# Order of high-part and low-part matmuls within a weight piece, and the place of the first down projection's last turns

## The chip, the core and the metric

The kernel runs on one core of one Trainium2 chip. The metric is the time of one execution on the device in microseconds (us), as the median of three runs; less is better. The engines of the core have queues of their own: TensorE multiplies matrices (PE in the profile; its weight loads are PEld), VectorE (DVE) and ScalarE (ACT) do elementwise work, GpSimd (POOL) and SyncE (SP) mostly issue DMA transfers. TensorE writes to PSUM, a memory of eight banks of 512 float32 per partition; everything else lies in SBUF.

## What is computed

The reference is a decoder trunk of two layers on one sequence of 256 tokens with 2048 features: a gated linear attention layer, then an attention layer over one block of shared keys and values, each followed by a gated feed-forward network with a short convolution.

```python
for layer in range(DEPTH):                     # DEPTH = 2
    if layer < N_A_LAYERS:
        h = h + gla_mixer(h, ...)
    else:
        if layer == N_A_LAYERS:
            k_blk, v_blk, k_mean = shared_kv(h, kv_norm, kv_w, k_norm_w)
        h = h + moba_mixer(h, ..., k_blk, v_blk, k_mean, rel_bias)
    h = h + conv_ffn(h, ...)                   # rms_norm, w_up, conv, silu(a) * u, w_down
```

Nearly all of the work is products of activations (256 tokens) with weight matrices: 2048 inputs to the several projections, 2048 to 2 x 5632 in each up projection, 5632 to 2048 in each down projection. All data is float32.

## The kernel before

**High and low parts.** Each float32 operand is used as a sum of two numbers of the matmul's input type: a high part (the rounded value) and a low part (what the rounding left). A product of two such operands is made of three: high x high, high x low, low x high. The activations lie as `[128, 2 * S]` per k-tile, high part in the first 256 columns, low part in the next 256 (`make_xw`, line 221). The weights come as pieces of `[128, 1024]` float32, half of a chunk of 2048 columns.

**The weight stream** (`WeightStream`, line 55). Chunks of 1 MB are fetched by DMAs on the SP queue into three buffers (`wraw`). For each piece ACT casts the high part (`whi`, line 126) and DVE subtracts it from the original to get the low part (`wlo`, line 127). There are three buffers each for `whi` and `wlo`, and pieces are prepared two ahead of the one in use. `step()` (line 289) hands out the next piece, and ahead of that runs the jobs that were put off with `after(n, job)` until n steps later.

**`gemm`** (line 298) has the weights as the stationary operand and the activations as the moving one. One step holds 4 k-tiles x 2 output blocks. For each of these 8 tiles there is one 512-wide matmul with `whi` against both parts of the activation (line 307), and one 256-wide matmul with `wlo` against the high part alone (line 308). It runs for the key, query, gate and output projections of the first layer, for both up projections, and for the output projection of the second layer: 120 calls of four steps, 480 steps in all. In the last step of a call the tiles of output block 0 come first.

**`gemm_tok`** (line 312) has the activations as the stationary operand and the weights as the moving one, three 512-wide matmuls per tile (lines 323 to 325): x high with w high, x high with w low, x low with w high. It makes the values of the first layer, and queries, keys and values of the second.

**`down`** (line 626) is the down projection, in two column blocks. Most input pairs use a scheme with seven products rather than eight of 2 x 2 blocks (`seven`), with sums and differences of weights and activations (`t13`, `t24` on DVE in `_sums`, lines 99 to 101; `comb` for the activations). `prod` (line 646) does one product as three 512-wide matmuls, in the order x high w high, x high w low, x low w high (line 653). Of a pair with seven products, the four weight pieces hold 1, 2, 2 and 2 of them. The results p1 to p8 lie in PSUM banks; p4 and p8 are in the two banks of the `bank` pool, the others in pairs in the `acc_ps` pool of three. The last pairs of a block (the tail) are run once per half `f`, and after each half `sums(f, ...)` adds the results to their buffers.

**The turns** (`back`, line 770). The first down projection gives its result with tokens on partitions; the kernel goes on with features on partitions. `back(q)` transposes block q of eight with four matmuls against the identity (line 777), adds it to the residual stream `h[q]` (line 779) and feeds the norm: `make_xw` (two casts on ACT, line 225, and two operations on DVE, line 227) and the square and its sum (lines 237 and 238). Turns 0 to 3 stand in the second block of `down`, turn 4 in its tail at (1, 1), all of them into an `acc_ps` tile, 5 to 7 in steps 1 to 3 of the first `gemm_tok` call of the queries, into the `bank` pool; `nrm.close`, which makes the norm's factor for each token, stands at step 4. Step q of that call uses the operand of turn q.

The program order is not the last word: a scheduler with a simulated timeline places the instructions on the queues of the engines, within what the data dependencies allow.

Of the kernel before, what the change touches and what calls it, by code (L numbers as in the profile page):

```python
# [8 lines left out]
F32 = mybir.dt.float32  # L9
# [9 lines left out]
S = 256  # L19
KT = D // 128  # L20
NP = KT // 2
# [121 lines left out]
def trunk(ctx: ExitStack, tc: tile.TileContext, xT, cst, msk, w1p, w2a, w_k, w_qa, w_v2, w_v, w_g, w_go,  # L143
          w_up0, w_dn0, w_kk, w_kv, w_mq, w_mo, w_up1, w_dn1, rel, onehot, out):
    nc = tc.nc
    V, A, T = nc.vector, nc.scalar, nc.tensor
# [7 lines left out]
    acc_ps = ctx.enter_context(tc.tile_pool(name="acc_ps", bufs=3, space=PSUM))  # L154
# [9 lines left out]
    def bank(name, shape):  # L164
        return mis_ps.tile(list(shape), F32, name=name, tag="bank")
# [117 lines left out]
    cur = [0]  # L283
    later = []

    def after(steps, job):
        later.append((cur[0] + steps, job))

    def step():
        due = [job for at, job in later if at <= cur[0]]  # L290
        later[:] = [(at, job) for at, job in later if at > cur[0]]
        for job in due:
            job()
        halves_ = ws.get(cur[0])
        cur[0] += 1
        return halves_

    def gemm(xs, kts):
        ps = acc_ps.tile([128, 2, 512], F32, name="acc")
        for q0 in range(0, kts, 4):  # L300
            hi, lo = step()
            order = [(k, b) for k in range(4) for b in range(2)]
            for k, b in sorted(order, key=lambda kb: kb[1]) if q0 == kts - 4 else order:
                kt = q0 + k
                x = xs(kt)
                c = k * 256 + b * 128
                T.matmul(ps[:, b, :], hi[:, c:c + 128], x, start=kt == 0, stop=False)  # L307
                T.matmul(ps[:, b, :S], lo[:, c:c + 128], x[:, :S], start=False, stop=kt == kts - 1)  # L308
        ws.prefetch(cur[0])
        return ps  # L310

    def gemm_tok(xs, groups=1):
        out_ = [acc_ps.tile([128, 2, 512], F32, name="acc") for _ in range(groups)]
        for q0 in range(0, KT, 2):
            for ps in out_:
                hi, lo = step()
                for k in range(2):
                    kt = q0 + k
                    x = xs(kt)
                    wh, wl = hi[:, k * 512:(k + 1) * 512], lo[:, k * 512:(k + 1) * 512]  # L320
                    for t in range(2):
                        xh, xl = x[:, 128 * t:128 * t + 128], x[:, S + 128 * t:S + 128 * t + 128]
                        T.matmul(ps[:, t, :], xh, wh, start=kt == 0, stop=False)  # L323
                        T.matmul(ps[:, t, :], xh, wl, start=False, stop=False)  # L324
                        T.matmul(ps[:, t, :], xl, wh, start=False, stop=kt == KT - 1)  # L325
        ws.prefetch(cur[0])
        return out_ if groups > 1 else out_[0]

# [41 lines left out]
    nrm = Norm(C_GN, "xw", columns=True)  # L370
# [7 lines left out]
    xs = rows(nrm.xs)  # L378
# [247 lines left out]
    def down(layer, hid, ready, jobs):  # L626

        def late(k):
            return lambda: combine_parts(k, hid)

        done = set(EARLY)
        for b, order in enumerate(ORDERS[layer]):
            new = [k for k, seven in order if seven and k not in done]
            done |= set(new)
            todo = dict(jobs.get(b, {}))
            for i, k in enumerate(new):
                todo.setdefault(2 + 2 * i, []).append(late(k))
            low = acc_ps.tile([128, 2, 512], F32, name="acc")
            p = {2: low[:, 0], 3: low[:, 1], 4: bank("p4", (128, 512)), 8: bank("p8", (128, 512))}
            left = dict.fromkeys(range(1, 9), 0)  # L640
            for k, seven in order:
                for n in ((1, 5, 7, 6, 4, 3, 2) if seven else (2, 3, 4, 8, 2, 3, 4, 8)):
                    left[n] += 3
            begun = set()

            def prod(n, x, w, f):
                hi, lo = (t[:, 512 * f:512 * f + 512] for t in w)
                if n not in p:
                    two = acc_ps.tile([128, 2, 512], F32, name="acc")
                    p.update({n: two[:, 0], {1: 6, 5: 7}[n]: two[:, 1]})  # L650
                for xp, wp in ((x[0], hi), (x[0], lo), (x[1], hi)):
                    left[n] -= 1
                    T.matmul(p[n], xp, wp, start=n not in begun, stop=left[n] == 0)  # L653
                    begun.add(n)

            def part(k, i, t):
                x = hid[k][:, i, 128 * t:]
                return x[:, :128], x[:, S:S + 128]

            def comb(k, f):  # L660
                return combos[k][:, f, 0], combos[k][:, f, 1]

            last = max(i for i, (k, seven) in enumerate(order) if seven)
            tail = [k for k, _ in order[len(order) - _tail(order):]]
            for i, (k, seven) in enumerate(order[:len(order) - len(tail)]):
                for job in todo.get(i, ()):
                    job()
                if seven:
                    prod(1, part(k, 0, 0), step(), 0)
                    w = step()  # L670
                    prod(3, comb(k, 3), w, 0)
                    prod(2, part(k, 1, 0), w, 1)
                    w = step()
                    prod(5, comb(k, 0), w, 0)
                    prod(7, comb(k, 2), w, 1)
                    w = step()
                    prod(6, comb(k, 1), w, 0)
                    prod(4, part(k, 1, 1), w, 1)
                else:
                    for a in range(2):  # L680
                        w = step()
                        for n, t, f in ((2, 0, a), (3, 0, 1 - a), (4, 1, a), (8, 1, 1 - a)):
                            prod(n, part(k, a, t), w, f)
                if i == last:
                    sums = ready(b, p)
            for f, (n0, n1) in enumerate(((2, 4), (3, 8))):
                for i, k in enumerate(tail):
                    for job in todo.get((f, i), ()):
                        job()
                    w = step()  # L690
                    todo_ = [(n, t, a) for a in range(2) for n, t in ((n0, 0), (n1, 1))]
                    for n, t, a in sorted(todo_, key=lambda x: x[1]) if i == len(tail) - 1 else todo_:
                        prod(n, part(k, a, t), w, a)
                if f:
                    ws.prefetch(cur[0])
                sums(f, (n0, n1))
# [61 lines left out]
    def first_down(hid, nrm):  # L758
        blocks = {}

        def ready(b, p):
            blocks[b] = r = u_sums(p, None)

            def end(c, ns):
                for t, n in enumerate(ns):
                    V.tensor_add(r[2 * t + c], r[2 * t + c], p[n])

            return end

        def back(q, where):  # L770

            r = blocks[q // 4]
            tp = where()
            c, i0 = q % 4 // 2, q % 2 * 2
            for i in range(2):
                for t in range(2):
                    T.transpose(tp[:, i, 128 * t:128 * t + 128],
                                r[2 * t + c][:, 128 * (i0 + i):128 * (i0 + i) + 128], ident)
            V.tensor_add(h[q], h[q], tp)
            nrm.feed(q)  # L780

        def load_back(m):
            hs[m] = slot([128, 2, 2, S], F32, "h")
            for q in (2 * m, 2 * m + 1):
                h[q] = hs[m][:, q % 2]
                nc.gpsimd.dma_start(h[q], hspill[q].rearrange("a (b c) -> a b c", b=2))

        pair = []

        def in_acc():  # L790
            if not pair:
                two = acc_ps.tile([128, 2, 512], F32, name="acc")
                pair.extend(two[:, i].rearrange("p (a b) -> p a b", a=2) for i in range(2))
            return pair.pop(0)

        jobs = {2: [lambda q=q: back(q, in_acc) for q in (0, 1)]}
        for q, i in ((2, 3), (3, 4), (4, (1, 1))):
            jobs.setdefault(i, []).append(lambda q=q: back(q, in_acc))
        for m, i in enumerate((0, 1, 15, 16)):
            jobs.setdefault(i, []).append(lambda m=m: load_back(m))  # L800
        down(0, hid, ready, {1: jobs})
        for q in (5, 6, 7):
            after(q - 4, lambda q=q: back(q, lambda: bank("hf", (128, 2, S))))
        after(4, nrm.close)

    n_ffn = Norm(C_FN, "xw")
    project(rows(go), KT, [n_ffn])
# [254 lines left out]
```

## Time and profile before

| what | value |
|---|---|
| median of three runs | 2245.56 us (2244.91 to 2245.88) |
| profiled execution, its own time | 2244.39 us |
| its span, first to last instruction | 2242.6 us |
| PE busy | 2226.1 us |
| DVE busy | 1659.1 us |
| ACT busy | 1260.5 us |
| matmuls | 11776 |

The profile is of one execution. Its page has the busy time of each engine, the span in 40 slices, the DMA queues, the chain of work that ended last (followed back from the last instruction to what released it), and the groups of instructions that cost most. Other views list the waits by who waited for whom, the instructions in order of time, and the sums over chosen windows of time. A row of instructions reads: start in us, duration in us, engine, line of the kernel, operation, tile written <- tiles read, shape. The duration of a matmul includes its way through the pipeline, so matmuls overlap in the rows: what a matmul costs in a stream is the distance from its start to the start of the next.

### The profile page before, as it was taken

To read this page: it belongs to the slowest core of one execution; us is meant where nothing else is said; L and a number is where in the kernel's file an instruction comes from. 1 tells how busy PE (TensorE), PEld (TensorE's weight loads), DVE (VectorE), ACT (ScalarE), POOL (GpSimd) and SP (SyncE) were. 2 spreads that over 40 slices of the span, in tenths; PEclk is the share of its full clock that TensorE was granted. 3 is DMA by queue.
4 is the path that set the end of the run, shared out by engine and by line. 5 is a ranking of instruction groups with operands and counts; after the bars stand their busy time and mean duration, and the time that the engine had idled before them with its cause. 6 is when DMAs were issued, how large, how long until landed. Compare 5 with 4: busy or idle time off the path is not lost.

```text
span 2242.6 us, 30203 instructions
## 1 busy us (share of the span) xinstructions
PE 2226.1 (99%) x11776; PEld 1901.9 (85%) x11776; DVE 1659.1 (74%) x2279; ACT 1260.5 (56%) x1754; POOL 44.1 (2%) x60
## 2 busy tenths in 40 slices
PE   8999999999999999999999999999999999999999
PEld 7889888888888888887788888888888888887877
DVE  6666776777777777978867666567777777788886
ACT  6655644655555555555556565456555555555553
POOL 0000000000000000000001000000000000000000
PEclk9999999999999999999999999999999999999999
DMA  6554556555555555555656554456655555556654
GB/s 257 188 188 135 172 194 210 191 188 188 188 188 187 184 183 198 197 196 192 226 185 218 177 169 158 165 191 205 202 188 188 189 189 192 192 195 209 242 194 146
DMA packets 63297, 428.50 MB, mean 191 GB/s; under 512 B 7553, under 2 KB 8081, under 8 KB 13106
## 3 DMA queue, kind: packets, MB, share of 16 engines
q1 hardware_dynamic: 59346, 415.43, 53.8%
q0 software_dynamic: 3232, 10.56, 1.4%
q8 instruction: 92, 1.51, 0.3%
q10 hardware_dynamic: 576, 0.58, 0.1%
q14 instruction: 51, 0.42, 0.1%
HBM read 420.23 MB, written 6.32 MB: 190 GB/s over the span
## 4 chain that ended last, share of the span: by engine, by line
PE 91%; DVE 4%; DMA 3%; issue 1%; ACT 1%; DVEq 0%; ACTq 0%
PE acc L307 40%; PE acc L308 20%; PE acc L653 8%; PE p L653 5%; PE acc L324 5%; PE acc L325 5%; PE acc L323 5%; DMA wraw<-w_dn 3%; DVE wlo L127 2%; ACT whi L126 1%; DVE t L99 1%; PE sT L511 0%; DMA wraw<-w_v 0%; PE tr L856 0%; PE s L874 0%
## 5 line engine op out<-in xcount | busy, mean ns | idle before, releaser
L127 DVE TENSOR_TENSOR wlo<-wraw,whi 128x1024 fp32r<-128x1024 f32 (+1 forms) x785 | 937.4, 1200 | 452.5 <-ACT whi L126 445.9
L126 ACT CAST whi<-wraw 128x1024 fp32r<-128x1024 f32 (+1 forms) x785 | 807.2, 1033 | 791.9 <-PE acc L307 465.8
L307 PE MATMUL acc<-xw,whi 128*128 128x512 f32 x3328 | 1168.4, 396 | 0.0
L308 PE MATMUL acc<-xw,wlo 128*128 128x256 f32 x3328 | 933.8, 281 | 0.0
L307 PEld LDWEIGHTS acc<-xw,whi 128*128 128x128 f32 x3328 | 624.2, 188 | 146.8
L308 PEld LDWEIGHTS acc<-xw,wlo 128*128 128x128 f32 x3328 | 628.8, 189 | 0.2
L653 PE MATMUL acc<-whi,hid 128*128 128x512 f32 x576 | 204.9, 390 | 0.1
L653 PE MATMUL p<-whi,hid 128*128 128x512 f32 x512 | 179.7, 390 | 0.0
L653 PEld LDWEIGHTS acc<-whi,hid 128*128 128x128 f32 x576 | 108.1, 188 | 22.8 <-ACT whi L126 0.5
L126 ACT CAST whi<-t 128x1024 fp32r<-128x1024 f32 x64 | 67.4, 1054 | 85.1 <-PE p L653 75.9
L653 PE MATMUL acc<-wlo,hid 128*128 128x512 f32 x288 | 113.0, 393 | 1.0 <-DVE wlo L127 0.8
L653 PEld LDWEIGHTS p<-whi,hid 128*128 128x128 f32 x512 | 96.1, 188 | 20.1
L323 PE MATMUL acc<-whi,xw 128*128 128x512 f32 x256 | 101.2, 396 | 5.0 <-ACT xw L225 5.0
L324 PE MATMUL acc<-wlo,xw 128*128 128x512 f32 x256 | 101.3, 396 | 0.9 <-DVE wlo L127 0.9
L324 PE MATMUL acc<-wlo,xkv 128*128 128x512 f32 x256 | 100.6, 393 | 0.0
L323 PE MATMUL acc<-whi,xkv 128*128 128x512 f32 x256 | 100.6, 393 | 0.0
L325 PE MATMUL acc<-whi,xw 128*128 128x512 f32 x256 | 100.5, 392 | 0.0
L325 PE MATMUL acc<-whi,xkv 128*128 128x512 f32 x256 | 100.4, 392 | 0.0
L610 ACT ACTIVATE au<-up,cs 128x256 f32<-128x256 f32 x176 | 96.0, 593 | 7.1 <-DVE up L606 7.1
L653 PE MATMUL p<-wlo,hid 128*128 128x512 f32 x256 | 99.7, 389 | 0.0
L127 DVE TENSOR_TENSOR wlo<-t,whi 128x1024 fp32r<-128x1024 f32 x64 | 77.9, 1222 | 23.7 <-ACT whi L126 23.3
L307 PE MATMUL acc<-go,whi 128*128 128x512 f32 x256 | 90.5, 399 | 0.0
(260 smaller groups left out, 2359.1 us busy)
## 6 DMA issues: line engine op xcount, KB each, us to landing
wraw<-w_up SPq DMA_DIRECT2D x176, 1024.0 KB, 4.8
wraw<-w_dn SPq DMA_DIRECT2D x88, 1024.0 KB, 4.9
wraw<-w_g SPq DMA_DIRECT2D x16, 1024.0 KB, 4.9
wraw<-w_go SPq DMA_DIRECT2D x16, 1024.0 KB, 4.8
wraw<-w_mq SPq DMA_DIRECT2D x16, 1024.0 KB, 4.8
wraw<-w_kk SPq DMA_DIRECT2D x16, 1024.0 KB, 4.8
wraw<-w_kv SPq DMA_DIRECT2D x16, 1024.0 KB, 4.8
wraw<-w_mo SPq DMA_DIRECT2D x16, 1024.0 KB, 4.8
```

Of the source, the lines that this page charges most:

```text
L99: V.tensor_sub(t13, src[:, 512:1536], src[:, 0:1024])
L126: nc.scalar.copy(hi[:, a:b], src[:, a:b])
L127: nc.vector.tensor_sub(lo[:, a:b], src[:, a:b], hi[:, a:b].bitcast(F32))
L307: T.matmul(ps[:, b, :], hi[:, c:c + 128], x, start=kt == 0, stop=False)
L308: T.matmul(ps[:, b, :S], lo[:, c:c + 128], x[:, :S], start=False, stop=kt == kts - 1)
L323: T.matmul(ps[:, t, :], xh, wh, start=kt == 0, stop=False)
L324: T.matmul(ps[:, t, :], xh, wl, start=False, stop=False)
L325: T.matmul(ps[:, t, :], xl, wh, start=False, stop=kt == KT - 1)
L610: A.activation(au[:, i, :], t[:, i, :], AF.Identity, bias=col(cb + n), scale=col(cw + 2 * 2 * FT + n))
L653: T.matmul(p[n], xp, wp, start=n not in begun, stop=left[n] == 0)
```

## The change

There are two parts. First, within each weight piece the matmuls with the high part of the weights all come ahead of those with the low part, in `gemm`, `gemm_tok` and `down`. In the last step of a `gemm` call this is done for output block 0 and then for block 1. In the first step of the program (`cur[0] == 1`) of `gemm_tok` it is done for each k-tile by itself. In `down`, `prods` takes all products of one piece and runs x high w high for all of them, then x low w high, then x high w low; the order by `t` in the last tail step is gone. Second, turn 4 moves from the tail of the first down projection to step 1 of the queries, turns 5 to 7 and the closing of the norm move back by one step each, and turn 4 now goes into the `bank` pool.

```diff
@@ gemm
-            order = [(k, b) for k in range(4) for b in range(2)]
-            for k, b in sorted(order, key=lambda kb: kb[1]) if q0 == kts - 4 else order:
-                kt = q0 + k
-                x = xs(kt)
-                c = k * 256 + b * 128
-                T.matmul(ps[:, b, :], hi[:, c:c + 128], x, start=kt == 0, stop=False)
-                T.matmul(ps[:, b, :S], lo[:, c:c + 128], x[:, :S], start=False, stop=kt == kts - 1)
+            for bs in ((0,), (1,)) if q0 == kts - 4 else ((0, 1),):
+                tiles_ = [(q0 + k, b, k * 256 + b * 128) for k in range(4) for b in bs]
+                for kt, b, c in tiles_:
+                    T.matmul(ps[:, b, :], hi[:, c:c + 128], xs(kt), start=kt == 0, stop=False)
+                for kt, b, c in tiles_:
+                    T.matmul(ps[:, b, :S], lo[:, c:c + 128], xs(kt)[:, :S], start=False, stop=kt == kts - 1)
@@ gemm_tok
-                for k in range(2):
...
-                        T.matmul(ps[:, t, :], xh, wh, start=kt == 0, stop=False)
-                        T.matmul(ps[:, t, :], xh, wl, start=False, stop=False)
-                        T.matmul(ps[:, t, :], xl, wh, start=False, stop=kt == KT - 1)
+                for ks in ((0,), (1,)) if cur[0] == 1 else ((0, 1),):
+                    tiles_ = [(q0 + k, t, k * 512) for k in ks for t in range(2)]
+                    for x0 in (0, S):
+                        for kt, t, c in tiles_:
+                            T.matmul(ps[:, t, :], xs(kt)[:, x0 + 128 * t:x0 + 128 * t + 128], hi[:, c:c + 512],
+                                     start=kt == 0 and x0 == 0, stop=False)
+                    for kt, t, c in tiles_:
+                        T.matmul(ps[:, t, :], xs(kt)[:, 128 * t:128 * t + 128], lo[:, c:c + 512],
+                                 start=False, stop=kt == KT - 1)
@@ down
-            def prod(n, x, w, f):
-                hi, lo = (t[:, 512 * f:512 * f + 512] for t in w)
...
-                for xp, wp in ((x[0], hi), (x[0], lo), (x[1], hi)):
-                    left[n] -= 1
-                    T.matmul(p[n], xp, wp, start=n not in begun, stop=left[n] == 0)
-                    begun.add(n)
+            def prods(*todo):
+
+                w = step()
+                for n, _, _ in todo:
+                    if n not in p:
+                        two = acc_ps.tile([128, 2, 512], F32, name="acc")
+                        p.update({n: two[:, 0], {1: 6, 5: 7}[n]: two[:, 1]})
+                for xi, wi in ((0, 0), (1, 0), (0, 1)):
+                    for n, x, f in todo:
+                        left[n] -= 1
+                        T.matmul(p[n], x[xi], w[wi][:, 512 * f:512 * f + 512], start=n not in begun, stop=left[n] == 0)
+                        begun.add(n)
...
-                    todo_ = [(n, t, a) for a in range(2) for n, t in ((n0, 0), (n1, 1))]
-                    for n, t, a in sorted(todo_, key=lambda x: x[1]) if i == len(tail) - 1 else todo_:
-                        prod(n, part(k, a, t), w, a)
+                    prods(*((n, part(k, a, t), a) for a in range(2) for n, t in ((n0, 0), (n1, 1))))
@@ first_down
-        for q, i in ((2, 3), (3, 4), (4, (1, 1))):
+        for q, i in ((2, 3), (3, 4)):
...
-        for q in (5, 6, 7):
-            after(q - 4, lambda q=q: back(q, lambda: bank("hf", (128, 2, S))))
-        after(4, nrm.close)
+        for q in range(4, NP):
+            after(q - 3, lambda q=q: back(q, lambda: bank("hf", (128, 2, S))))
+        after(5, nrm.close)
```

More of the change, by code (lines that the diff above doesn't have):

```diff
@@ L316, in gemm_tok @@
                 hi, lo = step()
-                for k in range(2):
[L318 to L325, printed above, removed]
+                for ks in ((0,), (1,)) if cur[0] == 1 else ((0, 1),):
[7 more added lines that the diff above has]
+                                 start=False, stop=kt == KT - 1)
         ws.prefetch(cur[0])
@@ L644, in down @@
             begun = set()
-            def prod(n, x, w, f):
-                hi, lo = (t[:, 512 * f:512 * f + 512] for t in w)
-                if n not in p:
-                    two = acc_ps.tile([128, 2, 512], F32, name="acc")
-                    p.update({n: two[:, 0], {1: 6, 5: 7}[n]: two[:, 1]})
-                for xp, wp in ((x[0], hi), (x[0], lo), (x[1], hi)):
-                    left[n] -= 1
-                    T.matmul(p[n], xp, wp, start=n not in begun, stop=left[n] == 0)
-                    begun.add(n)
+            def prods(*todo):
[9 more added lines that the diff above has]
+                        begun.add(n)
             def part(k, i, t):
@@ L668, in down @@
                 if seven:
[L669 to L678, printed above, removed]
+                    prods((1, part(k, 0, 0), 0))
+                    prods((3, comb(k, 3), 0), (2, part(k, 1, 0), 1))
+                    prods((5, comb(k, 0), 0), (7, comb(k, 2), 1))
+                    prods((6, comb(k, 1), 0), (4, part(k, 1, 1), 1))
                 else:
                     for a in range(2):
-                        w = step()
-                        for n, t, f in ((2, 0, a), (3, 0, 1 - a), (4, 1, a), (8, 1, 1 - a)):
-                            prod(n, part(k, a, t), w, f)
+                        prods(*((n, part(k, a, t), f)
+                                for n, t, f in ((2, 0, a), (3, 0, 1 - a), (4, 1, a), (8, 1, 1 - a))))
                 if i == last:
@@ L689, in down @@
                         job()
-                    w = step()
-                    todo_ = [(n, t, a) for a in range(2) for n, t in ((n0, 0), (n1, 1))]
-                    for n, t, a in sorted(todo_, key=lambda x: x[1]) if i == len(tail) - 1 else todo_:
-                        prod(n, part(k, a, t), w, a)
+                    prods(*((n, part(k, a, t), a) for a in range(2) for n, t in ((n0, 0), (n1, 1))))
                 if f:
```

## The prediction

> **What bounds the kernel now.** I read the page first: engine shares, the slices, the chain that ended last, the costliest groups.
>
> ```profile
> span 2242.6 us, 30203 instructions
> ...
> PE 2226.1 (99%) x11776; PEld 1901.9 (85%) x11776; DVE 1659.1 (74%) x2279; ACT 1260.5 (56%) x1754; POOL 44.1 (2%) x60
> ...
> PEclk9999999999999999999999999999999999999999
> ...
> PE 91%; DVE 4%; DMA 3%; issue 1%; ACT 1%; DVEq 0%; ACTq 0%
> ...
> L307 PE MATMUL acc<-xw,whi 128*128 128x512 f32 x3328 | 1168.4, 396 | 0.0
> L308 PE MATMUL acc<-xw,wlo 128*128 128x256 f32 x3328 | 933.8, 281 | 0.0
> ```
>
> TensorE matmul is busy 99% at full granted clock, 91% of the chain is its own, and its idle time is 2242.6 - 2226.1 = 16.5 us. The change keeps the number of matmuls. So it can act in two ways only: through the distance from one matmul to the next (the means of 396 and 281 ns overlap, they are not that distance), and through those 16.5 us.
>
> For the distance I took windows over two stages in which `gemm` runs almost alone, and divided time by the count of PE.
>
> ```profile
> core 0: us, PE busy (x) PEld busy (x) DVE busy (x) ACT busy (x) POOL busy (x), PEclk, DMA share, GB/s
> 240.00:880.00 640.00, 640.00 (x3627) 555.08 (x3626) 477.63 (x674) 360.53 (x499) 4.37 (x8) 1.00 0.56 190
> 1600.00:1960.00 360.00, 360.00 (x2079) 317.40 (x2078) 276.45 (x405) 206.40 (x296) 0.00 (x0) 1.00 0.56 190
> ```
>
> 640/3627 = 176.5 ns and 360/2079 = 173.2 ns per matmul: a pair of one 512-wide (high) and one 256-wide (low) matmul takes 353 ns in the first stage and 346 ns in the second, at the same clock. The alternating order therefore has at least two rhythms. A step of `gemm` has 8 pairs: 2.82 us or 2.77 us.
>
> For the idle time I asked the list of waits, and the groups of PE by form.
>
> ```profile
> ACT whi L126 <- PE p L653: 136.1, 86, 4.8
> ...
> DVE t L99 <- DMA wraw<-w_dn: 20.8, 16, 3.5
> ...
> PEld acc L653 <- DVE wlo L127: 12.8, 19, 1.6
> ...
> PE acc L653 <- DVE wlo L127: 5.6, 9, 1.1
> ```
>
> ```profile
> L653 PE MATMUL acc<-wlo,hid 128*128 128x512 f32 x288 | 113.0, 393 | 1.0 <-DVE wlo L127 0.8
> L324 PE MATMUL acc<-wlo,xw 128*128 128x512 f32 x256 | 101.3, 396 | 0.9 <-DVE wlo L127 0.9
> ...
> L653 PE MATMUL acc<-wlo,comb 128*128 128x512 f32 x128 | 50.8, 397 | 4.9 <-DVE wlo L127 4.9
> ```
>
> The stalls of TensorE outside the start are waits for the low part `wlo`, in the two down projections. That is where a later use of the low part can pay.
>
> **The change part by part. 1: gemm, 480 steps.** (16 k-tiles of 4 per step, 120 calls: 4+4+8+8+44 up to the first up projection, 8+44 later; 272 steps in the first rhythm, 208 in the second.) Eight alternating pairs become a run of eight 512-wide and a run of eight 256-wide matmuls. No instruction is added or removed; what is unknown is the distance inside the runs. The trace has both kinds of run elsewhere: the value matmuls (256-wide) that the queue put together, and `gemm_tok` matmuls (512-wide) right after 256-wide ones.
>
> ```profile
> 1398.15 0.28 PE L394 MATMUL o<-p,vm 128*128 128x256 f32 x1
> ...
> 1398.87 0.40 PE L324 MATMUL acc<-wlo,xkv 128*128 128x512 f32 x1
> ```
>
> ```profile
> 1406.66 0.28 PE L394 MATMUL o<-p,vm 128*128 128x256 f32 x1
> ...
> 1407.13 0.28 PE L396 MATMUL o<-p,vm 128*128 128x256 f32 x1
> ```
>
> ```profile
> 33.35 2.46 PE L417 MATMUL z<-xw,w1s 128*128 128x512 f32 x10
> ```
>
> ```profile
> 70.76 0.40 PE L431 MATMUL gk<-zst,w2t 81*128 81x256 f32 x2
> 71.00 0.40 PE L324 MATMUL acc<-wlo,xw 128*128 128x512 f32 x1
> ...
> 71.47 0.39 PE L323 MATMUL acc<-whi,xw 128*128 128x512 f32 x1
> ...
> 72.39 0.39 PE L324 MATMUL acc<-wlo,xw 128*128 128x512 f32 x1
> 72.62 0.39 PE L325 MATMUL acc<-whi,xw 128*128 128x512 f32 x1
> ```
>
> ```profile
> 920.46 2.27 PE acc L653 x10
> ```
>
> The low run: from 1398.15 six 256-wide ones, each with its own weight load, take 0.72 us (120 ns each); from 1406.66 four take 0.47 us (117 ns). Standing together costs nothing extra. Eight take 0.94 to 0.96 us, I take 0.95. The high run: right after a 256-wide matmul the 512-wide ones are slow at first (71.00 to 71.47: two distances of 235 ns) and then quiet (10 in 2.27 us in the chain of waits, 227 ns). Seven distances from 71.00 to 72.62 take 1.62 us, with an eighth of 0.23 it is 1.85; the ten from 33.35, also behind a narrow one, take 2.46 - 0.39 for nine distances, 230 ns, so 1.84 for eight. I take 1.845. A grouped step is 1.845 + 0.95 = 2.795 us. Against the first rhythm (2.823) that is -0.028 x 272 = -7.6 us, against the second (2.771) +0.024 x 208 = +5.0 us: the two nearly cancel, **-3 us** in all. Bound below: quiet throughout, 8 x (0.227 + 0.117) = 2.752, which against the mean of before, 2.800, is -0.048 x 480 = -23 us. Bound above: never quiet, 8 x (0.235 + 0.120) = 2.840, +0.040 x 480 = +19 us.
>
> The Trainium skill (TensorE: Matmul & The Clock Gate, "LDWEIGHTS (loading the stationary operand)") gives a weight load as columns / 1.2 in ns, by that an estimate of 107 ns for 128 columns, about as long as a 256-wide matmul streams, and in "Back-to-back issue gap" N/2.4 + 2.5 ns per matmul. By both, each matmul costs the same in either order (an estimate of 8 x 216 + 8 x 109 = 2.60 us per step), so part 1 would bring 0; the trace's 2.82 and 2.77 for the same work at the same clock do not agree with one fixed cost.
>
> **2: gemm_tok and down.** All their matmuls are 512-wide and stay so; rhythm unchanged, 0 us. No row shows this new order among equal widths; the quiet 227 ns of the chain and the 230 ns of the run at 33.35 are 3 ns apart, and a third of that on 3552 matmuls bounds it at -3.6 and +3.6 us (an estimate). What moves is the waiting. In a six-matmul step of `down` the low part was wanted second (high, low, high per product), now it is wanted fifth: three matmuls later, 3 x 0.23 = 0.68 us; in a step of three, 0.23 us. And `whi` is free for ACT after the fourth matmul rather than the sixth, while ACT waits 136.1 us in 86 times for just that. The 12.8 us in 19 waits are on average 0.67 us, the longest 1.6 us: most would vanish, the long ones halve. But PE's own idle time there is 4.9 + 1.0 = 5.9 us, and DVE's wait for w_dn (20.8 us, 16 times) stands ahead of some of them, which the order doesn't touch: what is late next is the sum `t` behind that DMA. I take **-5 us** (bounds 0, when the DMA sets the pace, and -12.8). In the first step of the program (`cur[0] == 1`), and at the end of the values, the 0.9 us of L324 shrink: **-0.4 us** (0 to -0.9).
>
> A new wait can arise where `down` passes to its second block: all four x-high products stand first, so the first use of bank p8 comes fourth, 3 x 0.23 = 0.68 us into the block, instead of tenth. The bank is read by the closing additions, as at the end of the kernel:
>
> ```profile
> 2237.63 0.39 PE L653 MATMUL p<-whi,hid 128*128 128x512 f32 x1
> 2237.83 0.69 DVE L745 TENSOR_TENSOR res<-res,acc 128x512 f32<-128x512 f32 x1 [7.25 <-PE acc L653]
> 2238.44 0.68 DVE L745 TENSOR_TENSOR res<-res,p 128x512 f32<-128x512 f32 x1
> ```
>
> The second addition ends at 2239.12, the first slot after the last matmul is 2237.86: 1.26 us, less 0.68 that lies beside matmuls: 0.6 us per passage, two passages; behind it stand all matmuls of the block. The queue may put ready products ahead, so I take **+0.6 us** (0 to +1.2). The dropped sorting of the last tail step costs nothing at the end: here too the last two matmuls belonged to different sums.
>
> **3: the moved turns.** Turn 4 goes from the tail to step 1 of the queries, 5 to 7 and the closing of the norm one step later each. No DMA is issued by them; the SP and POOL queues keep their order.
>
> ```profile
> 1135.50 0.87 DVE L227 SCALAR_TENSOR_TENSOR xw<-h,cs,xw 128x256 fp32r<-128x256 f32 x2
> 1135.56 0.59 PEld L777 LDWEIGHTS hf<-mk,c 128*128 128x128 f32 x4
> 1135.79 0.60 PE L777 MATMUL hf<-mk,c 128*128 128x128 f32 x4
> 1136.04 1.05 ACT L126 CAST whi<-wraw 128x1024 fp32r<-128x1024 f32 x1
> 1136.43 0.69 DVE L779 TENSOR_TENSOR h<-h,hf 128x512 f32<-128x512 f32 x1
> 1137.03 0.68 DVE L238 TENSOR_TENSOR acc_sq<-acc_sq,hsq 128x512 f32<-128x512 f32 x1
> ...
> 1137.63 1.22 DVE L127 TENSOR_TENSOR wlo<-wraw,whi 128x1024 fp32r<-128x1024 f32 x1
> ...
> 1146.48 0.64 PEld L272 LDWEIGHTS sum_h<-one,acc_sq 128*128 128x128 f32 x4
> ...
> 1151.54 0.68 ACT L840 ACTIVATE hsq<-acc,col_h 128x512 f32<-128x512 f32 x1
> ```
>
> PE's four transposes take the same 4 x 0.11 us in either place. DVE pays 0.69 + 0.87 + 0.68 = 2.24 us per turn beside a `wlo` of 1.22: 3.46 us in a step of 12 x 0.227 = 2.72 us, so it falls 0.74 us behind per turn, 3.0 us over four. The operand of turn q is wanted three steps later (8.2 us), so the lag is covered; without the cover it would be the 3.0 us. The sums for the closing ran 5 us ahead of the head norm (1146.5 to 1151.5) and may go 2.7 us later. **0 us** (0 to +3).
>
> Sum: -3 - 5 - 0.4 + 0.6 + 0 = -7.8. The profiled execution took 2244.39 us (span 2242.6 and 1.8 around it): 2236.6. The median of the runs is 2245.56, 1.2 above: **2238 us**.
>
> **The rivals.** A: the runs are quiet throughout, 2.75 per step: 2245.6 - 23 - 4.8 = 2218. The 227 and 117 ns do occur; against it, both quoted 512-wide runs behind a narrow matmul need some matmuls first. B: the mean distance doesn't depend on the order, only the waits fall: 2245.6 - 4.8 = 2241; against it stand the two rhythms of one and the same order. (B is what the rule of the Trainium skill above comes to.) C: it doesn't do what it says: the queue's order is made by a scheduler which already pulled high matmuls forward (at 2237.41 and 2237.63 two high ones end different sums), or the DMA sets the pace in down and the stalls only move: 2245. D, slower: the 512-wide ones never quiet down, because a narrow run follows every eight: 2.84 per step, 2245.6 + 19 - 4.8 = 2260; it turns slower by more than 0.2% from 2.82 per step on. For it, the first distances after a narrow run are 235 ns; against it, they fall within the seven that the rows show. E, slower: the turns in the queries come late, each up to one step of 2.72 us: +11, 2249 with the other gains; against it the 8.2 us of lead.
>
> **How the numbers follow.** Forecast 47%, A 15%, B 10%, C 8%, D 15%, E 5%. 0.2% (4.5 us) is about what this kernel's measurement can tell. Faster: 42 of the forecast's 47, A 15, half of B: 0.62. Within: 5, 5 and C's 8: 0.18. Slower: D and E: 0.20. The forecast's own range is 2230 to 2243 (stalls from -12.8 to 0 at the other terms' values); the range reaches into A and D until two in ten are out: 2222 to 2256.
>
> **What would show it.** Right: windows 240 to 880 and 1600 to 1960 give the same time per matmul, near 175 ns (2.795/16); the timeline shows eight L-high then eight L-low; `PEld acc <- DVE wlo` falls from 12.8 below 6 us; no wait of PE for h or xw in the queries. Wrong: a time per matmul above 176 ns in both stages (D), below 173 (A), PE idle unchanged at 16.5 us (C).

## The result and the profile after

| | before | changed |
|---|---|---|
| median | 2245.72 us (2244.91 to 2246.40, 4 runs) | 2228.85 us (2227.11 to 2229.33, 4 runs) |
| ratio | | 0.9924, 95% interval 0.9906 to 0.9941 |
| span of the profiled execution | 2242.6 us | 2227.3 us |

The changed kernel is faster by 16.9 us in the medians and by 15.3 us in the two profiled spans. The forecast was 2238 us, a gain of 8: the direction and the range (2222 to 2256) hold, the size is about half of what came.

First the page of the changed kernel, with busy times, chain, the two groups of `gemm` (L305, L307) and the first of `gemm_tok` (L320).

```profile
span 2227.3 us, 30386 instructions
...
PE 2217.3 (100%) x11776; PEld 1908.2 (86%) x11776; DVE 1647.8 (74%) x2279; ACT 1266.6 (57%) x1754; POOL 44.1 (2%) x60
...
PE 96%; DMA 2%; DVE 1%; issue 1%; ACT 0%; DVEq 0%; ACTq 0%
...
L305 PE MATMUL acc<-xw,whi 128*128 128x512 f32 x3328 | 854.4, 393 | 0.0
...
L307 PE MATMUL acc<-xw,wlo 128*128 128x256 f32 x3328 | 481.6, 282 | 0.0
...
L320 PE MATMUL acc<-whi,xw 128*128 128x512 f32 x512 | 130.2, 395 | 5.1 <-ACT xw L225 5.1
```

The idle time of PE fell from 16.5 to 2227.3 - 2217.3 = 10.0 us; half of that is the 5.1 us in which the first matmul waits for the first activation (L320). The busy time of L305 looks 314 us smaller than that of L307 of before (1168.4), yet no work left: a group's busy time is the time that its own matmuls cover, overlaps counted once, and eight of a kind in a row overlap one another, where before each overlapped its neighbours of the other line. It can't be used for what a matmul costs; the windows can, with the same two stretches as before:

```profile
core 0: us, PE busy (x) PEld busy (x) DVE busy (x) ACT busy (x) POOL busy (x), PEclk, DMA share, GB/s
240.00:880.00 640.00, 640.00 (x3664) 562.39 (x3663) 478.35 (x684) 367.73 (x505) 4.37 (x8) 1.00 0.56 191
1600.00:1960.00 360.00, 360.00 (x2062) 316.37 (x2061) 270.23 (x399) 206.69 (x292) 0.00 (x0) 1.00 0.55 188
```

640/3664 = 174.7 and 360/2062 = 174.6 ns per matmul: one rhythm in both stages, 349.2 ns per pair, 2.79 us per step. The prediction had 2.795 us and 174.7 ns. The first stage gained on 176.5, the second lost on 173.2.

The timeline of PE shows the runs of eight (an `x8` row is eight matmuls merged, its duration goes from the first start to the last end):

```profile
600.50 2.00 PE L305 MATMUL acc<-xw,whi 128*128 128x512 f32 x8
602.34 1.11 PE L307 MATMUL acc<-xw,wlo 128*128 128x256 f32 x8
603.29 2.00 PE L305 MATMUL acc<-xw,whi 128*128 128x512 f32 x8
```

Eight high ones from 600.50 to 602.34 take 1.84 us, eight low ones from 602.34 to 603.29 take 0.95: the two terms that the prediction read from other matmuls.

The waits, and the groups of PE by form that read a low part:

```profile
ACT whi L126 <- PE p L655: 88.1, 63, 4.4
...
DVE t L99 <- DMA wraw<-w_dn: 27.6, 16, 4.0
...
ACT whi L126 <- PE acc L655: 23.2, 29, 3.5
...
PEld acc L655 <- DVE wlo L127: 2.7, 6, 0.9
```

```profile
L655 PE MATMUL acc<-wlo,hid 128*128 128x512 f32 x288 | 95.7, 390 | 0.6 <-DVE wlo L127 0.5
...
L323 PE MATMUL acc<-wlo,xw 128*128 128x512 f32 x256 | 70.2, 394 | 0.0
...
L655 PE MATMUL acc<-wlo,comb 128*128 128x512 f32 x128 | 44.4, 390 | 0.1
```

The wait of the weight loads for the low part went from 12.8 to 2.7 us, below the 6 that the prediction named as its sign. The idle time ahead of the low parts went from 4.9 + 1.0 + 0.9 = 6.8 us to 0.7. DVE waits longer for the weights of the down projection than before (27.6 instead of 20.8 us), and TensorE hardly feels it.

Where the 15.3 us of span came from, by the starts of the first matmul of each stage in the two timelines:

| stage | before, us | changed, us | difference |
|---|---|---|---|
| start, values, keys, queries, gate | 300.99 | 298.26 | -2.7 |
| output projection, first layer | 90.46 | 89.46 | -1.0 |
| first up projection | 497.71 | 492.45 | -5.3 |
| first down, queries, keys, values | 531.19 | 525.71 | -5.5 |
| output projection, second layer | 91.27 | 91.78 | +0.5 |
| second up projection | 492.45 | 495.99 | +3.5 |
| second down, to the end | 238.53 | 233.65 | -4.9 |

### The profile page after: what moved, and what is told of

It reads as the page before. It is cut to its first block, busy times and chain, and to the rows that moved or that the text cites. A ratio compares the mean times of both kernels' runs of the same rounds, so it can differ in the third digit from the quotient of the medians.

```text
span 2227.3 us, 30386 instructions
## 1 busy us (share of the span) xinstructions
PE 2217.3 (100%) x11776; PEld 1908.2 (86%) x11776; DVE 1647.8 (74%) x2279; ACT 1266.6 (57%) x1754; POOL 44.1 (2%) x60
## 4 chain that ended last, share of the span: by engine, by line
PE 96%; DMA 2%; DVE 1%; issue 1%; ACT 0%; DVEq 0%; ACTq 0%
PE acc L305 40%; PE acc L307 21%; PE acc L655 11%; PE acc L320 11%; PE p L655 7%; PE acc L323 5%; DMA wraw<-w_dn 2%; DVE wlo L127 1%; PE sT L510 0%; PE tr L848 0%; PE s L866 0%; PE pT L886 0%; DVE t L100 0%; PE z L416 0%; PE s L864 0%
## 5 line engine op out<-in xcount | busy, mean ns | idle before, releaser
L305 PE MATMUL acc<-xw,whi 128*128 128x512 f32 x3328 | 854.4, 393 | 0.0
L305 PEld LDWEIGHTS acc<-xw,whi 128*128 128x128 f32 x3328 | 590.8, 189 | 98.8
L307 PEld LDWEIGHTS acc<-xw,wlo 128*128 128x128 f32 x3328 | 468.4, 190 | 41.7
L307 PE MATMUL acc<-xw,wlo 128*128 128x256 f32 x3328 | 481.6, 282 | 0.0
L320 PE MATMUL acc<-whi,xw 128*128 128x512 f32 x512 | 130.2, 395 | 5.1 <-ACT xw L225 5.1
L320 PE MATMUL acc<-whi,xkv 128*128 128x512 f32 x512 | 133.6, 394 | 0.0
L320 PEld LDWEIGHTS acc<-whi,xw 128*128 128x128 f32 x512 | 96.4, 190 | 25.1 <-ACT xw L225 5.1
L320 PEld LDWEIGHTS acc<-whi,xkv 128*128 128x128 f32 x512 | 94.3, 188 | 18.4
L655 PE MATMUL acc<-whi,comb 128*128 128x512 f32 x256 | 83.4, 389 | 0.0
L613 DVE SCALAR_TENSOR_TENSOR au<-up,cs,au 128x254 f32<-128x254 f32 x176 | 77.3, 477 | 0.0
L611 DVE SCALAR_TENSOR_TENSOR au<-up,cs,au 128x255 f32<-128x255 f32 x176 | 76.8, 477 | 0.0
```

What stands on the lines that cost most here:

```text
L305: T.matmul(ps[:, b, :], hi[:, c:c + 128], xs(kt), start=kt == 0, stop=False)
L307: T.matmul(ps[:, b, :S], lo[:, c:c + 128], xs(kt)[:, :S], start=False, stop=kt == kts - 1)
L320: T.matmul(ps[:, t, :], xs(kt)[:, x0 + 128 * t:x0 + 128 * t + 128], hi[:, c:c + 512], start=kt == 0 and x0 == 0, stop=False)
L611: V.scalar_tensor_tensor(au[:, i, 1:], t[:, i, :S - 1], col(cw + 2 * FT + n), au[:, i, 1:], op0=OP.mult, op1=OP.add)
L613: V.scalar_tensor_tensor(au[:, i, 2:], t[:, i, :S - 2], col(cw + n), au[:, i, 2:], op0=OP.mult, op1=OP.add)
L655: T.matmul(p[n], x[xi], w[wi][:, 512 * f:512 * f + 512], start=n not in begun, stop=left[n] == 0)
```

## The experiments: each part by itself

The first four kernels are the kernel before with one part of the diff each (the hunks are those shown with the change).

**Only gemm.** The hunk of `gemm` alone.

> The kernel before with the new order in gemm alone. Theory (each part of the change works by itself): a gemm step is 2.795 us wherever it stands, so 640 us from 240 to 880 hold about 3664 matmuls and 360 us from 1600 to 1960 about 2062; the stages up to the first down get 9 us shorter, those of the second layer's output and up projections 4 us longer, sum -5 us: about 2241; the waits of the down projections stay (PEld acc on DVE wlo 12 to 13 us). Rival (all of the gain is rhythm, also carried into the down projections): 2229 to 2233.

Measured: 2242.58 us, before 2246.77 on the same chip, ratio 0.9982 (0.9973 to 0.9992); span 2239.7. Its windows and its list of waits:

```profile
240.00:880.00 640.00, 640.00 (x3666) 562.35 (x3666) 477.33 (x682) 368.86 (x505) 4.39 (x8) 1.00 0.56 191
1600.00:1960.00 360.00, 360.00 (x2062) 316.28 (x2061) 271.89 (x402) 208.35 (x294) 0.00 (x0) 1.00 0.55 188
```

```profile
PEld acc L652 <- DVE wlo L127: 13.2, 18, 1.9
```

The counts are as expected to two matmuls, the waits in the down projections are untouched. By stages: -7.7 us up to the first down, +4.0 in the second layer: -3.7 us; by the medians -4.2. The rival, that the rhythm makes all of the gain, falls.

**Only down.** The hunk of `down` alone.

> The kernel before with the new order in down alone. Theory: the gain of the two down projections (5.5 and 4.9 us in the trace of the changed kernel) is of the order of parts: -10 us, about 2235, waits of PEld acc on DVE wlo below 4 us, gemm unchanged at 2.82 and 2.77 us per step. Rival (half of it came from the turn that left the tail, or from the phase in which the gemm ahead ends): -3 to -6 us, about 2241.

Measured: 2233.02 us, before 2246.77, ratio 0.9938 (0.9921 to 0.9955); span 2233.4, 9.2 us below that of before.

```profile
DVE t L99 <- DMA wraw<-w_dn: 25.9, 15, 3.2
...
PEld acc L656 <- DVE wlo L127: 4.1, 7, 1.3
```

The wait for the low part falls from 12.8 to 4.1 us. From its first to its last matmul the first down took 231.56 us instead of 236.89, the second 230.29 instead of 233.56. By the medians this hunk brings 13.7 us, by the spans 9.2, of the changed kernel's 16.9 and 15.3; the rival (-3 to -6 us) falls. The two measures differ because a span is of one execution: that of before took 2244.39 us, less than the median of its kernel on this chip (2246.77), and that of this run 2235.21, the most of its four.

**Only the moved turns.**

> The kernel before with the last turns moved and nothing else. Theory: 0 us, 2245 to 2246.5, no wait of PE in the queries. Rival (the turn in the tail held up the first down): -3 to -5 us. Second rival (turns late in the queries): +3 us or more.

Measured: 2246.53 us, before 2246.77, ratio 1.0002 (0.9993 to 1.0012); span 2242.7. Nothing either way. Its waits in the down projections stay:

```profile
PEld acc L653 <- DVE wlo L127: 13.7, 19, 2.6
```

In the changed kernel these rows show how near the later place comes to costing something: the sums for the norm's factor, the factor on POOL, and the head norm on ACT that reads it.

```profile
1134.56 0.64 PEld L272 LDWEIGHTS sum_h<-one,acc_sq 128*128 128x128 f32 x4
...
1135.56 0.72 POOL L280 TENSOR_TENSOR col_h<-mean_h,mhalf 128x2 f32<-128x2 f32 x1 [74.24 <-DVE mean_h L279]
1136.32 0.69 ACT L832 ACTIVATE hsq<-acc,col_h 128x512 f32<-128x512 f32 x1 [0.52 <-POOL col_h L280]
```

Before, the sums ran 5 us ahead of their reader; now the reader waits 0.52 us for them. It is ACT that waits, beside TensorE's next group, so the time doesn't show it.

**Only gemm_tok.**

> The kernel before with the new order in gemm_tok alone. Theory: only the wait in the first microseconds goes, -0.5 to -1.5 us, about 2245; the stage of the queries and that of keys and values keep their lengths (93.0 and 201.0 us) to 0.3 us. Rival (the order among matmuls of one width changes their distance): up to 3.6 us either way.

Measured: 2246.70 us, before 2246.77, ratio 1.0002 (0.9992 to 1.0011). In its trace the first layer's output projection starts 1.0 us earlier (300.01 instead of 300.99), which fits the wait of the start; but with the turns alone, where nothing ahead of that point is changed, it starts at 300.25, so one trace doesn't settle it. The rest of the run gave it back (span 2244.8): the second layer's output projection took 92.7 us instead of 91.3, the first down 0.6 and the second 0.9 us more. Whether the expected gain of a microsecond is there stays open; the medians don't show it. The rival of a new distance among equal widths has no support: from the first matmul of the queries to the last of keys and values it is 293.8 us in both traces.

By the medians the four parts bring 4.2 + 13.7 + 0.2 + 0.1 = 18.2 us, the whole change 16.9: the parts add up to it about as well as medians tell.

## The experiments: why the wait in down goes

The new order does two things at once: the low part is wanted later, and the high part is given back sooner, so that ACT may cast the next one sooner. Two orders in `down` alone part them; the diffs are against the hunk of `down` and show the order only.

```diff
-                for xi, wi in ((0, 0), (1, 0), (0, 1)):
-                    for n, x, f in todo:
...
+                order_ = ([(0, 0, j) for j in range(m)] + [(1, 0, j) for j in range(m - 1)]
+                          + [(0, 1, j) for j in range(m)] + [(1, 0, m - 1)])
+                for xi, wi, j in order_:
+                    n, x, f = todo[j]
...
```

> The kernel before with a new order in down alone: all x high w high, then x low w high but for the last product, then all low parts, then the last x low w high. The low part is wanted nearly as late as in the changed kernel (fourth of six instead of fifth), but whi is held to the end of the piece, as before. Theory 1 (the gain is that the low part is wanted later, two to three matmuls or 0.45 to 0.68 us per wait): -7 to -9 us, about 2237, PEld acc on DVE wlo below 6 us. Theory 2 (the gain is that whi is given back earlier and ACT casts earlier): 0 to -2 us, about 2246, the wait stays at 12 to 13 us.

```diff
...
+                order_ = ([(0, 0, 0), (0, 1, 0)] + [(0, 0, j) for j in range(1, m)] + [(1, 0, j) for j in range(m)]
+                          + [(0, 1, j) for j in range(1, m)])
...
```

> The kernel before with a new order in down alone: first product's x high w high and x high w low, then all other matmuls with the high part, then the other low parts. The low part is wanted second, as before; whi is given back after the fifth of six (ninth of twelve) instead of the last. Theory 1 (late use is what pays): 0 to -2 us, about 2246, PEld acc on DVE wlo 11 to 13 us. Theory 2 (early return of whi pays): -6 to -9 us, about 2238, the wait below 6 us.

Late use measured 2238.07 us, early return 2236.08 us, before 2247.53 on the same chip; ratios 0.9958 (0.9943 to 0.9973) and 0.9949 (0.9934 to 0.9963). The waits of late use:

```profile
ACT whi L126 <- PE p L659: 132.8, 85, 5.1
...
ACT whi L126 <- PE acc L659: 42.1, 51, 4.2
...
DVE t L99 <- DMA wraw<-w_dn: 22.3, 18, 3.2
PEld acc L659 <- DVE wlo L127: 7.9, 12, 2.0
```

and of early return:

```profile
ACT whi L126 <- PE acc L659: 132.6, 120, 5.3
...
ACT whi L126 <- PE p L659: 23.1, 11, 4.8
DVE t L99 <- DMA wraw<-w_dn: 16.2, 13, 3.6
...
PEld acc L659 <- DVE wlo L127: 4.7, 9, 1.4
```

and one more row of the kernel before:

```profile
ACT whi L126 <- PE acc L653: 41.2, 42, 4.2
```

Neither theory stands alone. ACT's waits for the buffer are the `p` and the `acc` row together: 136.1 + 41.2 = 177.3 us before, 174.9 with late use, 155.7 with early return, 111.3 in the changed kernel. Late use leaves them as they were and takes the wait for the low part from 12.8 to 7.9 us. Early return, with the low part wanted second as before, takes it to 4.7 us: more, though the prediction had put no price on it. In the medians late use brings 9.5 us and early return 11.4, and each execution of early return is quicker than each of late use; the whole hunk brought 13.7 on another chip, with an interval that overlaps both. So each alone brings most of the gain, and the two overlap.

## The experiments: the rhythm of gemm

The alternating order was quicker than the runs of eight in the second layer. This kernel keeps the change, but alternates there (`project(rows(ox), ...)` and the up projection of layer 1).

```diff
...
-                for kt, b, c in tiles_:
+                for some in [[t] for t in tiles_] if alternate else [tiles_]:
+                    for kt, b, c in some:
...
```

> The changed kernel, but gemm in its old alternating order in the second layer (output projection and up projection). Theory (the alternating order has two rhythms, and in the second layer it falls into the quicker one, 346.6 ns per pair against 349.2 in runs of eight): those two stages get 4.0 us shorter, about 2225 where the changed kernel is 2229. Rival (the quick rhythm was luck of the phase in which those stages began, and the new order ahead of them ends in another phase): the stages fall into 353 ns, +5 to +6 us against the changed kernel.

Measured: 2225.59 us, before 2247.53, ratio 0.9902 (0.9885 to 0.9918). By the interval it can't be told from the changed kernel; the trace shows the difference:

```profile
240.00:880.00 640.00, 640.00 (x3664) 562.28 (x3664) 478.81 (x684) 367.85 (x504) 4.38 (x8) 1.00 0.56 191
1600.00:1960.00 360.00, 360.00 (x2079) 317.44 (x2078) 275.90 (x401) 206.42 (x295) 0.00 (x0) 1.00 0.56 190
```

The window from 1600 is back at 2079 matmuls. The up projection took 492.7 us (496.0 in the changed kernel), but the output projection 92.7 (91.8): there the alternation fell into the slow rhythm, where before it had mostly been in the quick one. The run with `gemm_tok` alone did the same without any change in `gemm`: in 50 us of that stage it has 285 matmuls (first view), the kernel before 290 (second).

```profile
1440.00:1490.00 50.00, 50.00 (x285) 43.31 (x284) 32.42 (x38) 23.54 (x30) 0.00 (x0) 1.00 0.56 190
```

```profile
1440.00:1490.00 50.00, 50.00 (x290) 43.70 (x289) 34.02 (x42) 25.60 (x34) 0.00 (x0) 1.00 0.56 190
```

Both theories are half right: the same matmuls of the same stage run in either rhythm, by what ran ahead of them.

Next, runs of eight only in the first step of each call, to set the phase.

```diff
...
+                for some in [[t] for t in tiles_] if q0 else [tiles_]:
...
```

> The changed kernel, but in gemm only the first step of each call runs its high and low parts in runs of eight; the other three steps alternate. Theory A (a run of 256-wide matmuls sets the phase, and the alternation behind it takes up the quick rhythm): 346.6 ns per pair in those steps everywhere, 640 us from 240 to 880 hold about 3685 matmuls, the kernel about 2222. Theory B (the phase is set otherwise, the first layer keeps its slow rhythm): 353 ns per pair there, about 3640 matmuls, 2232 to 2236.

One execution: 2237.51 us, span 2235.7.

```profile
240.00:880.00 640.00, 640.00 (x3637) 557.11 (x3636) 478.57 (x677) 365.57 (x502) 4.37 (x8) 1.00 0.56 190
1600.00:1960.00 360.00, 360.00 (x2046) 313.34 (x2045) 273.28 (x399) 205.51 (x291) 0.00 (x0) 1.00 0.54 186
```

640/3637 = 176.0 ns, and from 1600 on 360/2046 = 176.0 ns: the slow rhythm, now in both layers. A run of eight sets the phase, but to the slow side. The timelines gave a hint for the other side: in the kernel before two 512-wide matmuls of the second layer's output projection stood side by side (the `x2` row), at the point of the slow rhythm where the distance is 241 ns, and behind them the rhythm was quick.

```profile
1433.60 0.64 PE L307 MATMUL acc<-ox,whi 128*128 128x512 f32 x2
```

The last kernel puts such a pair into the second step of each call.

```diff
...
+            order = {0: "HHHHHHHHllllllll", 4: "HlHHlHlHlHlHlHll"}.get(q0, "HlHlHlHlHlHlHlHl")
+            todo = {"H": list(tiles_), "l": list(tiles_)}
+            for part in order:
+                kt, b, c = todo[part].pop(0)
...
```

> The changed kernel, but in gemm the first step of each call runs eight high, then eight low; in the second step the order is H l H H l H l H l H l H l H l l (H high, l low), with two high ones together at the third and fourth place; all others alternate. Theory A (the rhythm of the alternation is a phase that two 512-wide matmuls in a row, put where the distance is 241 ns, bring into the quick state, and that then holds): 346.6 ns per pair from the second step on, 640 us from 240 to 880 hold about 3685 matmuls, -6 to -8 us against the changed kernel of the same call. Theory B (the slow rhythm belongs to the first layer's operands): 353 ns, +6 to +9 us.

> The changed kernel itself once more, on the same chip as the run beside it, as its measure: 2227 to 2231 us, 349.2 ns per pair in the steps with runs of eight.

Measured on one chip: 2220.0 us with the pair, 2228.19 us the changed kernel, before 2245.47; ratios 0.9889 (0.9875 to 0.9902) and 0.9921 (0.9907 to 0.9934). The intervals don't overlap. This is the fastest of all. Windows, and the timeline of PE around the pair:

```profile
240.00:880.00 640.00, 640.00 (x3680) 561.12 (x3679) 486.97 (x688) 371.21 (x509) 4.38 (x8) 1.00 0.56 193
1600.00:1960.00 360.00, 360.00 (x2074) 315.77 (x2073) 276.16 (x401) 208.25 (x295) 0.00 (x0) 1.00 0.55 190
```

```profile
600.32 0.40 PE L310 MATMUL acc<-xw,whi 128*128 128x512 f32 x1
600.56 0.28 PE L312 MATMUL acc<-xw,wlo 128*128 128x256 f32 x1
600.67 0.64 PE L310 MATMUL acc<-xw,whi 128*128 128x512 f32 x2
601.15 0.28 PE L312 MATMUL acc<-xw,wlo 128*128 128x256 f32 x1
601.27 0.39 PE L310 MATMUL acc<-xw,whi 128*128 128x512 f32 x1
...
602.31 0.39 PE L310 MATMUL acc<-xw,whi 128*128 128x512 f32 x1
```

Behind the pair (the `x2` row) three pairs of high and low take 602.31 - 601.27 = 1.04 us, 347 ns each, in the first layer, where the old order took 353. 640/3680 = 173.9 ns includes the run of eight at the head of each call. Theory A stands: the same operands run in either rhythm, and the pair brings the quick one.

## Why the prediction was half right

The direction came out right, and by the two mechanisms that were forecast. The size did not: 2228.85 us lies 1 us below the forecast's own bounds (2230 to 2243) and within the stated range only because that was widened for the rivals A and D, neither of which came. That the range holds is in part luck.

**Part 1, the distance in gemm: right.** -3 us was forecast, -3.7 us measured by the stages with that part alone (-4.2 in the medians), and each of its two halves had the forecast sign and size (-7.6 and +5.0; measured -7.7 and +4.0). The step of 2.795 us, read from a few matmuls of other lines, was met to 0.2%. The Trainium skill's fixed costs per matmul (TensorE: Matmul & The Clock Gate, "Back-to-back issue gap") would have given no change in either stage; the runs show one loss and one gain, so a single cost per width doesn't do here.

**Part 2, the waits in down: right in kind, and the term that was mis-sized.** Forecast -5 us; measured -5.5 and -4.9 in the two stages that hold a down projection; with this part alone -5.3 and -3.3 from first to last matmul, and -13.7 in the medians. Three readings failed.

The first was the size of the loss: it went by PE's idle time of 5.9 us, and took the DMA for a brake on the rest. But a matmul's tail counts as busy while the next one waits, and the distance behind a wait is longer too, so idle time undercounts a late operand. One wait of the kernel before:

```profile
2024.31 0.62 PE L653 MATMUL acc<-whi,hid 128*128 128x512 f32 x2
2025.83 0.50 PE L653 MATMUL acc<-wlo,comb 128*128 128x512 f32 x1 [0.91 <-DVE wlo L127]
2026.17 0.40 PE L653 MATMUL acc<-whi,comb 128*128 128x512 f32 x1
```

The second of the first two starts at 2024.54. From there to 2026.17 it is 1.63 us where two quiet distances are 0.45: 1.18 us are lost, and 0.91 are booked as idle. The second down of before has 1008 matmuls, 233.56 us from the first start to the last; 1007 quiet distances of 0.227 us are 228.6: 5.0 us lost in one of two, 4.8 of them in 16 distances above 0.3 us, so they are waits and not a slower rhythm. The changed kernel's 229.16 leaves 0.6. Over all traces the second down takes 233.5 to 234.5 us with the old order of `down` (four traces) and 228.8 to 232.2 with the new one (six), so a difference of 2 us between two single traces means little.

The second was the list of steps. The prediction priced steps of six and of three matmuls, and the text ahead of it says that most input pairs use seven products; by `ORDERS` it is 8 of the 22 of a block. The other 14 have steps of twelve matmuls, two thirds of all of `down`: there the low part goes from second to ninth place, 7 x 0.227 = 1.6 us later, and `whi` comes back after the eighth matmul instead of the twelfth. What these steps are worth by themselves was not measured.

The third was the mechanism's other half: that `whi` returns sooner stood in the text without a price, and by the runs it is at least as strong as the later use (11.4 against 9.5 us in the medians). That the DMA would set the pace is refuted by the wait of DVE for it, which grew to 27.6 us while TensorE's wait went.

**The start:** -0.4 forecast, about -1.0 us in the trace of `gemm_tok` alone, hardly more than the 0.7 us by which that stretch differs between traces that have it unchanged. **The new wait for bank p8:** +0.6 forecast, none found: in the trace of the changed kernel TensorE makes no pause at the passage between the blocks. Whether the scheduler's order hides it was not tried. **The turns:** 0 forecast, 0 measured; the cover that was named (5 us of lead of the norm's factor) is used up, as the 0.52 us wait of ACT shows.

**The rivals.** A, runs quiet throughout, did not come: its low run was to take 117 ns per matmul, the eight low ones in 0.95 us take 119; its high run 227 ns, and eight high ones in 1.84 us take 230, because a run begins slowly: over 331 runs of the trace the first two distances are 233.5 and 235.5 ns in the mean, the last three 227. B is refuted by the windows (176.5 to 174.7 and 173.2 to 174.6 ns per matmul) and by `gemm` alone, whose interval ends below 1, D by the eight high ones in 1.84 us, E by the run with the turns alone. C is refuted in both its halves: in `gemm` the order on PE is the one written, and the waits in down went instead of moving.

## What to carry to other kernels

Where an engine is nearly always busy, take what a late operand costs from starts: the number of matmuls in the stage at their quiet distance, against its length. Idle time shows only a part. When an operand is reordered, price both ends of it, when it is first wanted and when its buffer comes back. And order among matmuls of mixed widths is worth a trial by itself, judged by the count in a fixed window, which tells 1 ns per matmul where medians can't tell 2 us. The length of a stage with waits is another matter: between single traces of the same order it differed by more than 3 us, so there medians decide.

## What the hardware showed that was not expected

The same alternating matmuls have two states that last for hundreds of microseconds at the same full clock. The timeline of the kernel before in the slow one, then in the quick one, three pairs each:

```profile
299.93 0.40 PE L307 MATMUL acc<-xw,whi 128*128 128x512 f32 x1
...
300.99 0.40 PE L307 MATMUL acc<-go,whi 128*128 128x512 f32 x1
```

```profile
1700.05 0.39 PE L307 MATMUL acc<-xw,whi 128*128 128x512 f32 x1
...
1701.09 0.39 PE L307 MATMUL acc<-xw,whi 128*128 128x512 f32 x1
```

1.06 against 1.04 us. In the slow state the distances go round in three pairs (233, 117, 241, 120, 236, 113 ns), in the quick one they are 230 and 117 ns throughout. Transposes that stand in between move the sequence in some places from one state to the other; two 512-wide matmuls side by side behind the 117 of the slow round moved it to the quick state in each of the 110 calls of `gemm` in which no other matmul came between (the four pairs behind the doubled one average 346 to 347 ns in all of them). What in the chip holds the state was not tried and stays open.
